# Turned tiles of a two-layer decoder trunk: one write to DRAM each in place of four, and VectorE's 32 x 32 squares taken from every fourth column

## The chip, the cores and the metric

The kernel runs on one core of a Trainium2 chip. The metric is the device time of one execution in microseconds (us). Engines are named as the profile names them: PE is TensorE, DVE is VectorE, ACT is ScalarE, POOL is GpSimd, and SP is SyncE, which here issues transfers and computes nothing. A transfer (DMA) is issued by SP, ACT or POOL and carried out by the core's 16 DMA engines.

## The reference

One sequence of 256 tokens with a width of 2048 goes through two layers in fp32. Each layer is a token mixer and an MLP, both behind an RMSNorm, both adding into the residual x:

```
h = rms_norm(x, mix_norm_g[i])
mix = fox_attention(h, ...) if i % 2 == 0 else dilated_attention(h, ...)
x = x + mix
h = rms_norm(x, mlp_norm_g[i])
a = relu(h @ w_up)               # 2048 -> 8192
x = x + (a * a) @ w_down         # 8192 -> 2048
```

The first mixer is causal softmax attention with 16 heads of 128 and a forget-gate bias. The second mixes three groups of 8 heads, each over a dilated window, with shared values. In both, q and k are normalised per head of 128 and scaled by a gain per column. Nearly all arithmetic lies in matrix products of 256 tokens with weights that are read from DRAM once.

## The kernel before

**Products.** Tokens lie in two tiles of 128 (`t`), columns in chunks of 512 (`NC`). To keep fp32 accuracy every operand is split in a rounded part (`wh`, `hT`, `aTh`) and the rest (`wl`, `aTl`), and each product is three matmuls: high x high, high x low, low x high (lines 471 to 473; in the wide products 1198 to 1200). A weight unit is 256 rows x 512 columns. SP loads it into a `raw` tile, ACT rounds it into `wh` (line 417) and DVE subtracts to get `wl` (line 418). There are five `wh` and five `wl` tiles, so ACT and DVE can be at most five units ahead of PE. In the up projections of the MLPs some pairs of column chunks are computed together, in what the code calls "wide" products: seven block products in place of eight, for which DVE also forms sums and differences of weights (`sd`, `v`, lines 414, 420 and 421). Such a unit costs DVE more than a plain one.

**Turning.** A product needs its left operand with the contracted dimension on the partitions, so activations are transposed between products. After the first norm, tiles are turned without PE. DVE's transpose takes a 128 x 512 tile as 32 x 32 squares: a square stays on its 32 partitions. To move it to other partitions, the tile is written to DRAM in four transfers, one for each 32 partitions, and read back by one transfer in which a partition reads 2 KB in one run. This is done in four places: the norms before the MLPs and the second mixer (`transposed_by_dma`, transpose on line 571), q and k (`qk_chain`, line 748), the softmax weights (`p_turned`, line 819, tiles of 128 x 384), and the squared activations of both MLPs (`turn_up`, line 1119). In the first three, SP issues the writes and the read, by `move`. In `turn_up` POOL issues the writes (line 1113) and SP the read. What comes back is split by ACT (line 1144) and DVE (lines 1148 and 1151) into `aTh` and `aTl`.

**Gains.** `more_constants` loads the gains of q and k (8 rows of 128) and of the MLP norms (32 rows) as rows, PE turns them into columns (line 212), DVE copies them to `gain` (line 213).

**Order.** The order on each engine is the order in which the program is written. `Jobs` weaves it: the products call `jobs.tick()` after every 128 rows of weights, and a chain such as `turn_up` is a generator that gives the number of ticks, or the event, after which it goes on. The same ticks hold before and after the change. Every engine works its queue in order; an instruction that waits holds up those behind it. In the order of DVE a transpose of `turn_up` stands between the weight splits, as in:

```
for t in range(NT):
    tiles.append(work.tile([P, NC], F32, tag="w", name=f"turned_{key}_{n}_{t}", bufs=6))
    nc.vector.transpose(...)      # DVE, line 1119
    if t:
        write(t - 1)              # POOL, line 1113
    yield 1                       # one tick: about six matmuls, and a weight split behind each second
```

Of the kernel before, what the change touches and what calls it, by code (L numbers as in the profile page):

```python
# [137 lines left out]
def trunk(ctx: ExitStack, tc, x, fox_w_in, fox_b_f, fox_q_gain, fox_k_gain, fox_w_out, dil_w_in,  # L138
# [94 lines left out]
    def more_constants():  # L233
        yield 5
        wf = work.tile([P, KC, FH], F32, tag="t2", name="wf")
        nc.sync.dma_start(wf, fox_w_in[0][:, 3 * D:3 * D + FH].rearrange("(c p) n -> p c n", p=P))
        nc.sync.dma_start(bf, fox_b_f.to_broadcast([P, FH]))
        rows = gain_rows("g_rest", [fox_q_gain, fox_k_gain, dil_q_gain[0], dil_k_gain[0],
                                    mlp_norm_g.rearrange(per_chunk, p=P)])
        di = distances()  # L240
        yield 9
        nc.scalar.copy(wfs[:, :, 0:FH], wf)
        nc.vector.tensor_sub(wfs[:, :, FH:2 * FH], wf, wfs[:, :, 0:FH].bitcast(F32))
        jobs.done.add("wf")
        yield 1
        gain_columns("g_rest", rows, FOX_G)
        for c in (FOX_G, DIL_G, DIL_G + 1, DIL_G + 2):
            nc.vector.tensor_scalar_mul(gain[:, c:c + 1], gain[:, c:c + 1], SCALE)
        yield 1
        mask = work.tile([P, 3 * P], F32, tag="t0", name="mask")  # L250
        nc.vector.tensor_copy(mask, di)
        nc.vector.tensor_scalar(mask, mask, 0.0, None, ALU.is_ge)
        nc.vector.tensor_scalar(mask, mask, BIG, -BIG, ALU.mult, ALU.add)
        tables["mask"] = mask
        jobs.done.add("mask")
# [117 lines left out]
    def move(dst, src):  # L373

        nc.sync.dma_start(dst, src)

    state = {"raw": 0, "split": 0}
    pooled, corners = [0], {"free": False, "users": []}
# [179 lines left out]
    def transposed_by_dma(tag, col, n):  # L558
# [3 lines left out]
        for t in range(NT):  # L562
# [4 lines left out]
                tile_ = both.rearrange("p a b -> p (a b)")[:, t * NC:(t + 1) * NC]  # L567
            else:
                tile_ = work.tile([P, NC], F32, tag="w", name=f"turned_{tag}_{n}_{t}", bufs=6)
            blocks = dram.tile([4, 32, 4, P], F32, tag="blocks", name=f"blocks_{tag}_{n}_{t}", bufs=4)  # L570
            nc.vector.transpose(tile_.rearrange("p (j b r) -> p b j r", j=4, b=4),
                                xt[n][:, t, :].rearrange("p (b j c) -> p b j c", j=4, c=32))
            for i in range(4):
                move(blocks[:, :, i, :].rearrange("j c x -> c j x"),
                     tile_[32 * i:32 * i + 32].rearrange("p (j x) -> p j x", j=4))
            tiles.append((tile_, blocks))
        yield 3
        for tile_, blocks in tiles:
            move(tile_, blocks.rearrange("j c i x -> (j c) (i x)"))
        yield 11 if n else 9  # L580
        for half in range(2):
            pr = n * 2 + half
# [140 lines left out]
    def qk_chain(acc, tag, key, parts):  # L723
# [17 lines left out]
        for t in range(NT):  # L741
# [7 lines left out]
            blocks = dram.tile([4, 32, 4, P], F32, tag="blocks", name=f"blocks_{key}_{t}", bufs=4)  # L749
            for i in range(4):  # L750
                move(blocks[:, :, i, :].rearrange("j c x -> c j x"), sq[t][32 * i:32 * i + 32].rearrange("p (j x) -> p j x", j=4))
            qn.append(q)
            turns.append(blocks)
            yield 2
        yield 1
        for t in range(NT):
            yield 2 * t
            move(qn[t], turns[t].rearrange("j c i x -> (j c) (i x)").rearrange("p (h d) -> p h d", h=4))
        yield clear(6)
        for t in range(NT):  # L760
            subs = []
# [53 lines left out]
    def p_turned(p, name, landing):  # L815


        turned = work.tile([P, 4, 3, 32], F32, tag="s", name=f"turned_{name}", bufs=S_BUFS)
        nc.vector.transpose(turned.rearrange("p j b r -> p b j r"), p.rearrange("p (b j c) -> p b j c", b=3, c=32))
        blocks = dram.tile([4, 32, 4, 3 * 32], F32, tag="pblocks", name=f"pblocks_{name}", bufs=4)  # L820
        for i in range(4):
            move(blocks[:, :, i, :].rearrange("j c x -> c j x"),
                 turned[32 * i:32 * i + 32].rearrange("p j b r -> p j (b r)"))
        yield 5
        move(turned.rearrange("p i b r -> p (i b r)"), blocks.rearrange("j c i x -> (j c) (i x)"))
        yield clear(landing)
        return turned

# [274 lines left out]
    def turn_up(rows, key, n, aT, free=None, behind=None):  # L1103
# [5 lines left out]
        held, tiles = [], []  # L1109

        def write(t):
            for i in range(4):
                nc.gpsimd.dma_start(held[t][:, :, i, :].rearrange("j c x -> c j x"),
                                    tiles[t][32 * i:32 * i + 32].rearrange("p (j x) -> p j x", j=4))

        for t in range(NT):
            tiles.append(work.tile([P, NC], F32, tag="w", name=f"turned_{key}_{n}_{t}", bufs=6))
            held.append(dram.tile([4, 32, 4, P], F32, tag="held", name=f"held_{key}_{n}_{t}", bufs=16))
            nc.vector.transpose(tiles[t].rearrange("p (j b r) -> p b j r", j=4, b=4),
                                rows[t].rearrange("p (b j c) -> p b j c", j=4, c=32))  # L1120
            if t:
                write(t - 1)
            yield 1
# [5 lines left out]
        for t in range(NT):  # L1129
            yield 1  # L1130
            back.append(work.tile([P, NC], F32, tag="w", name=f"back_{key}_{n}_{t}", bufs=6))
            move(back[t], held[t].rearrange("j c i x -> (j c) (i x)"))
        yield clear(more(6, "turned", *at, 2))
        if free:
            yield free
# [242 lines left out]
```

## Time and profile before

Three runs gave a median of 2074.55 us (2074.14 to 2074.99). The profiled execution took 2072.56 us itself; its trace spans 2070.5 us.

| | before |
|---|---|
| median of the runs | 2074.55 us |
| profiled execution | 2072.56 us, span 2070.5 us |
| PE busy | 2064.7 us |
| DVE busy | 1782.1 us, of which 96 to 99% in parts of the MLPs |
| ACT busy | 1328.4 us |
| POOL busy | 247.6 us |
| transfers | 549.51 MB, mean 265 GB/s |

Rows of a timeline give the start, the duration, the engine, the line of the kernel, the operation, and `out<-in` by the program's names. Rows of a group give the count (x), then the busy time in us, the mean duration of one in ns, and the idle time of the engine just before them. Rows of a window table give the busy time in that stretch, the number of instructions (x), the granted clock of PE, the share of DMA time and the rate of the transfers. Matmuls are pipelined: one of 512 columns is shown with 0.38 us, and the next one starts 0.215 or 0.216 us after it. So PE counts as busy also across a short wait, and a short wait shows only in the distance between two starts. The time from one stage of the trace to another is told by lines: lines 571 belong to norms, 748 and 819 to the mixers, 1119 to the MLPs (`n1` is the first MLP, `n3` the second).

### The profile page before, as it was taken

How to read it: one execution, taken by the hardware profiler on the slowest of the kernel's cores; microseconds unless marked ns; L12 is line 12 of the kernel's file. 1: busy time of each engine (PE TensorE's matmuls, PEld its weight loads, DVE VectorE, ACT ScalarE, POOL GpSimd, SP SyncE). 2: the span in 40 equal slices, each digit the busy share in tenths (PEclk: the TensorE clock that was granted, in tenths of full speed). 3: DMA queues.
4: the chain of work that ended last, by engine and by line, in shares of the span. 5: the costliest groups of instructions: out<-in, count | busy, mean ns of one | idle time of the engine just before them, and what ended most of it. 6: DMA issues, size and time to landing. Idle time of an engine off the chain costs nothing.

```text
span 2070.5 us, 29000 instructions
## 1 busy us (share of the span) xinstructions
PE 2064.7 (100%) x9790; PEld 1813.2 (88%) x9790; DVE 1782.1 (86%) x2283; ACT 1328.4 (64%) x1833; POOL 247.6 (12%) x367
## 2 busy tenths in 40 slices
PE   9999999999999999999999999999999999999999
PEld 7888888888888888888888888888888888888888
DVE  6888876899999999997768787767999899999984
ACT  6665654867676676765656565555866676676673
POOL 1000000022020211211010010000112020120230
PEclk9999999999999999999999999999999999999999
DMA  8888887889898989989877876877888898899995
GB/s 259 258 260 263 258 249 217 268 284 293 267 298 266 290 271 300 306 256 283 287 240 233 251 234 216 255 217 241 263 288 284 270 298 265 280 292 295 292 280 187
DMA packets 355924, 549.51 MB, mean 265 GB/s; under 512 B 43496, under 2 KB 131904, under 8 KB 355776
## 3 DMA queue, kind: packets, MB, share of 16 engines
q1 hardware_dynamic: 336512, 511.28, 76.5%
q0 software_dynamic: 18560, 35.67, 7.4%
q8 instruction: 76, 1.25, 0.2%
q10 hardware_dynamic: 704, 0.72, 0.1%
q14 instruction: 72, 0.59, 0.1%
HBM read 488.29 MB, written 40.39 MB: 255 GB/s over the span
## 4 chain that ended last, share of the span: by engine, by line
PE 99%; DMA 0%; SPq 0%; DVE 0%; issue 0%
PE acc L471 25%; PE acc L472 25%; PE acc L473 25%; PE wide_n_tp L1199 3%; PE wide_n_tp L1200 3%; PE wide_n_tp L1198 3%; PE wide_n_sc L1199 2%; PE wide_n_acc L1198 2%; PE wide_n_acc L1200 2%; PE wide_n_sc L1200 2%; PE wide_n_acc L1199 2%; PE wide_n_sc L1198 2%; PE sc_d L859 0%; PE sc_f L859 0%; PE po_f L808 0%; PE po_d L808 0%
## 5 line engine op out<-in xcount | busy, mean ns | idle before, releaser
L418 DVE TENSOR_TENSOR wl<-raw,wh 128x1024 fp32r<-128x1024 f32 (+1 forms) x755 | 910.0, 1213 | 227.8 <-ACT wh L417 219.6
L417 ACT CAST wh<-raw 128x1024 fp32r<-128x1024 f32 (+1 forms) x755 | 782.0, 1044 | 424.5 <-PE acc L473 333.2
L471 PE MATMUL acc<-wh,hT_n 128*128 128x512 f32 x864 | 328.7, 380 | 0.0
L472 PE MATMUL acc<-wl,hT_n 128*128 128x512 f32 x864 | 327.9, 379 | 0.0
L473 PE MATMUL acc<-wh,hT_n 128*128 128x512 f32 x864 | 327.8, 379 | 0.0
L472 PE MATMUL acc<-wl,aTh_n1a 128*128 128x512 f32 x512 | 194.2, 379 | 0.0
L471 PE MATMUL acc<-wh,aTh_n1a 128*128 128x512 f32 x512 | 194.2, 379 | 0.0
L473 PE MATMUL acc<-wh,aTl_n1a 128*128 128x512 f32 x512 | 194.2, 379 | 0.0
L417 ACT CAST wh<-sd 128x1024 fp32r<-128x1024 f32 x96 | 100.7, 1049 | 139.9 <-DVE sd L414 129.0
L473 PEld LDWEIGHTS acc<-wh,hT_n 128*128 128x128 f32 x864 | 163.5, 189 | 22.9
L472 PEld LDWEIGHTS acc<-wl,hT_n 128*128 128x128 f32 x864 | 163.7, 189 | 22.1 <-DVE wl L418 0.3
L471 PEld LDWEIGHTS acc<-wh,hT_n 128*128 128x128 f32 x864 | 163.6, 189 | 21.8
L473 PE MATMUL acc<-wh,aTl_n3a 128*128 128x512 f32 x480 | 182.1, 379 | 0.0
L471 PE MATMUL acc<-wh,aTh_n3a 128*128 128x512 f32 x480 | 182.1, 379 | 0.0
L472 PE MATMUL acc<-wl,aTh_n3a 128*128 128x512 f32 x480 | 182.1, 379 | 0.0
L1051 POOL DMA_DIRECT2D x<-y_n x72 | 64.0, 927 | 638.8 <-ACT y_n L1050 637.0
L417 ACT CAST wh<-v 128x1024 fp32r<-128x1024 f32 x96 | 100.7, 1048 | 44.2 <-PE acc L473 22.2
L418 DVE TENSOR_TENSOR wl<-v,wh 128x1024 fp32r<-128x1024 f32 x96 | 116.7, 1216 | 5.5 <-ACT wh L417 5.4
L418 DVE TENSOR_TENSOR wl<-sd,wh 128x1024 fp32r<-128x1024 f32 x96 | 116.7, 1216 | 0.0
L414 DVE TENSOR_TENSOR sd<-raw,raw 128x1024 f32<-128x1024 f32 x96 | 116.6, 1214 | 0.0
L471 PE MATMUL acc<-wh,hc_n 128*128 128x512 f32 x288 | 109.4, 380 | 0.0
L472 PE MATMUL acc<-wl,hc_n 128*128 128x512 f32 x288 | 109.3, 379 | 0.0
(679 smaller groups left out, 3913.8 us busy)
## 6 DMA issues: line engine op xcount, KB each, us to landing
raw<-in_mlp_w_up_dram SPq DMA_DIRECT2D x304, 512.0 KB, 5.1
raw<-in_mlp_w_down_dram SPq DMA_DIRECT2D x256, 512.0 KB, 5.4
raw<-in_dil_w_in_dram SPq DMA_DIRECT2D x192, 256.0 KB, 3.5
raw<-in_fox_w_in_dram SPq DMA_DIRECT2D x95, 512.0 KB, 4.9
x<-y_n POOLq DMA_DIRECT2D x72, 256.0 KB, 6.5
raw<-in_fox_w_out_dram SPq DMA_DIRECT2D x32, 512.0 KB, 4.8
raw<-in_dil_w_in_dram SPq DMA_DIRECT2D x32, 512.0 KB, 4.7
raw<-in_dil_w_out_dram SPq DMA_DIRECT2D x32, 512.0 KB, 4.4
```

The source lines that it names most:

```text
L414: nc.vector.tensor_sub(quarters[0], raw, raws[n - 1][:, 1, :].unsqueeze(1).to_broadcast([P, RAW_SUB, NC]))
L417: nc.scalar.copy(hi[:, part, :], raw[:, part, :])
L418: nc.vector.tensor_sub(lo[:, part, :], raw[:, part, :], hi[:, part, :].bitcast(F32))
L471: nc.tensor.matmul(acc[t], ah, hi, start=first, stop=False)
L472: nc.tensor.matmul(acc[t], ah, lo, start=False, stop=False)
L473: nc.tensor.matmul(acc[t], al, hi, start=False, stop=last)
L1051: nc.gpsimd.dma_start(xt[n][:, t, :], y, accum_op=ALU.add)
L1198: nc.tensor.matmul(banks[bank], ah, wh, start=what < 3 and of == 0, stop=False, **alone)
L1199: nc.tensor.matmul(banks[bank], ah, wl, start=False, stop=False, **alone)
L1200: nc.tensor.matmul(banks[bank], al, wh, start=False, stop=of == KC // 2 - 1, **alone)
```

## The change

In all four places the tile is now written to DRAM in one transfer of 128 partitions x 2 KB (1.5 KB for the softmax weights), as it lies. The reading transfer does the sorting: a partition reads four pieces of 512 bytes (384 for the softmax weights) that lie 32 rows apart. Read this way, partition p gets what came from old partitions with the index 4c + j in place of 32j + c. To have the columns in their old order, DVE's transpose now takes as one square's columns every fourth column of a 128-column block (`(b c j)` in place of `(b j c)`), on lines 571, 819 and 1119. For q and k the transpose on line 748 stays as it was, and the columns of a head come out in another order, the same one for q and k. Their gains are put in that order once: two small copies of DVE through a tile `spread`.

```diff
+        spread = work.tile([8, P], F32, tag="s", name="spread", bufs=S_BUFS)
+        nc.vector.tensor_copy(spread.rearrange("n (c j) -> n c j", j=4), rows[0:8].rearrange("n (j c) -> n c j", j=4))
+        nc.vector.tensor_copy(rows[0:8], spread)
         gain_columns("g_rest", rows, FOX_G)
...
+    def scratch(tag, name, width=P, bufs=4):
+        return dram.tile([P, 4 * width], F32, tag=tag, name=name, bufs=bufs)
+
+    def turned_back(blocks):
+        return blocks.rearrange("(i c) (j x) -> (c j) i x", i=4, j=4)
...
# transposed_by_dma
-            blocks = dram.tile([4, 32, 4, P], F32, tag="blocks", name=f"blocks_{tag}_{n}_{t}", bufs=4)
+            blocks = scratch("blocks", f"blocks_{tag}_{n}_{t}")
             nc.vector.transpose(tile_.rearrange("p (j b r) -> p b j r", j=4, b=4),
-                                xt[n][:, t, :].rearrange("p (b j c) -> p b j c", j=4, c=32))
-            for i in range(4):
-                move(blocks[:, :, i, :].rearrange("j c x -> c j x"),
-                     tile_[32 * i:32 * i + 32].rearrange("p (j x) -> p j x", j=4))
+                                xt[n][:, t, :].rearrange("p (b c j) -> p b j c", j=4, c=32))
+            move(blocks, tile_)
...
-            move(tile_, blocks.rearrange("j c i x -> (j c) (i x)"))
+            move(tile_.rearrange("p (i x) -> p i x", i=4), turned_back(blocks))
...
# qk_chain
-            for i in range(4):
-                move(blocks[:, :, i, :].rearrange("j c x -> c j x"), sq[t][32 * i:32 * i + 32].rearrange("p (j x) -> p j x", j=4))
+            move(blocks, sq[t])
...
# p_turned
-        nc.vector.transpose(turned.rearrange("p j b r -> p b j r"), p.rearrange("p (b j c) -> p b j c", b=3, c=32))
+        nc.vector.transpose(turned.rearrange("p j b r -> p b j r"), p.rearrange("p (b c j) -> p b j c", b=3, c=32))
...
# turn_up
-            for i in range(4):
-                nc.gpsimd.dma_start(held[t][:, :, i, :].rearrange("j c x -> c j x"),
-                                    tiles[t][32 * i:32 * i + 32].rearrange("p (j x) -> p j x", j=4))
+            nc.gpsimd.dma_start(held[t], tiles[t])
...
             nc.vector.transpose(tiles[t].rearrange("p (j b r) -> p b j r", j=4, b=4),
-                                rows[t].rearrange("p (b j c) -> p b j c", j=4, c=32))
+                                rows[t].rearrange("p (b c j) -> p b j c", j=4, c=32))
...
-            move(back[t], held[t].rearrange("j c i x -> (j c) (i x)"))
+            move(back[t].rearrange("p (i x) -> p i x", i=4), turned_back(held[t]))
```

No instruction of PE is added or removed, and the splits keep their order. POOL's order at the start of the first MLP, before the change; `held_n1a` is the DRAM copy of a turned tile, `x<-y` the added output of a down projection:

```order
L1113 DMA held_n1a_2_0_4582<-turned_n1a_2_0_4581 32x4x128 x4
L1113 DMA held_n1a_2_1_4600<-turned_n1a_2_1_4599 32x4x128 x4
L1113 DMA held_n1a_3_0_4877<-turned_n1a_3_0_4876 32x4x128 x4
L1113 DMA held_n1a_3_1_4890<-turned_n1a_3_1_4889 32x4x128 x4
L1051 DMA x_103<-y_n_0_0_194_5161 128x512
```

and with it:

```order
L1116 DMA held_n1a_2_0_4453<-turned_n1a_2_0_4452 128x512
L1116 DMA held_n1a_2_1_4471<-turned_n1a_2_1_4470 128x512
L1116 DMA held_n1a_3_0_4742<-turned_n1a_3_0_4741 128x512
L1116 DMA held_n1a_3_1_4755<-turned_n1a_3_1_4754 128x512
L1055 DMA x_103<-y_n_0_0_194_5020 128x512
```

Each write is one row in place of four (x4), at the same place. DVE's order about 29 us into the program, before the change, where it copies the turned gains out of PSUM (the brackets name what an instruction waits for):

```order
L418 TENSOR_TENSOR wl_384<-raw_245,wh_383 128x1024 [waits DMAHW1_49,Activation_49]
L243 TENSOR_TENSOR wfs<-wf,wfs 128x16x16 [waits DMAHW2_49,Activation_49]
L213 COPY gain<-ps_g_rest 128x40 [waits PE_49]
L248 TENSOR_SCALAR gain<-gain 128x1 [waits DVE_49]
L248 TENSOR_SCALAR gain<-gain 128x1 x3
```

and with it:

```order
L427 TENSOR_TENSOR wl_384<-raw_245,wh_383 128x1024 [waits DMAHW1_49,Activation_49]
L243 TENSOR_TENSOR wfs<-wf,wfs 128x16x16 [waits DMAHW2_49,Activation_49]
L247 COPY spread<-g_rest 8x128 [waits DMAHW6_49,DMAHW7_49,DMAHW5_49,DMAHW4_49]
L248 COPY g_rest<-spread 8x128 [waits DVE_49]
L213 COPY gain<-ps_g_rest 128x40 [waits PE_49]
```

The two copies stand ahead of the copy out of PSUM, and PE's transpose of the gains (line 212) now waits for them.

More of the change, by code (lines that the diff above doesn't have):

```diff
@@ L748, in qk_chain @@
             nc.vector.transpose(turned.rearrange("p j h r -> p h j r"), q.rearrange("p h (j c) -> p h j c", c=32))
-            blocks = dram.tile([4, 32, 4, P], F32, tag="blocks", name=f"blocks_{key}_{t}", bufs=4)
-            for i in range(4):
-                move(blocks[:, :, i, :].rearrange("j c x -> c j x"), sq[t][32 * i:32 * i + 32].rearrange("p (j x) -> p j x", j=4))
+            blocks = scratch("blocks", f"blocks_{key}_{t}")
+            move(blocks, sq[t])
             qn.append(q)
@@ L757, in qk_chain @@
             yield 2 * t
-            move(qn[t], turns[t].rearrange("j c i x -> (j c) (i x)").rearrange("p (h d) -> p h d", h=4))
+            move(qn[t], turned_back(turns[t]))
         yield clear(6)
@@ L818, in p_turned @@
         turned = work.tile([P, 4, 3, 32], F32, tag="s", name=f"turned_{name}", bufs=S_BUFS)
-        nc.vector.transpose(turned.rearrange("p j b r -> p b j r"), p.rearrange("p (b j c) -> p b j c", b=3, c=32))
-        blocks = dram.tile([4, 32, 4, 3 * 32], F32, tag="pblocks", name=f"pblocks_{name}", bufs=4)
-        for i in range(4):
-            move(blocks[:, :, i, :].rearrange("j c x -> c j x"),
-                 turned[32 * i:32 * i + 32].rearrange("p j b r -> p j (b r)"))
+        nc.vector.transpose(turned.rearrange("p j b r -> p b j r"), p.rearrange("p (b c j) -> p b j c", b=3, c=32))
+        blocks = scratch("pblocks", f"pblocks_{name}", 3 * 32)
+        move(blocks, turned.rearrange("p j b r -> p (j b r)"))
         yield 5
-        move(turned.rearrange("p i b r -> p (i b r)"), blocks.rearrange("j c i x -> (j c) (i x)"))
+        move(turned.rearrange("p i b r -> p i (b r)"), turned_back(blocks))
         yield clear(landing)
@@ L1111, in write @@
         def write(t):
-            for i in range(4):
-                nc.gpsimd.dma_start(held[t][:, :, i, :].rearrange("j c x -> c j x"),
-                                    tiles[t][32 * i:32 * i + 32].rearrange("p (j x) -> p j x", j=4))
+            nc.gpsimd.dma_start(held[t], tiles[t])
         for t in range(NT):
             tiles.append(work.tile([P, NC], F32, tag="w", name=f"turned_{key}_{n}_{t}", bufs=6))
-            held.append(dram.tile([4, 32, 4, P], F32, tag="held", name=f"held_{key}_{n}_{t}", bufs=16))
+            held.append(scratch("held", f"held_{key}_{n}_{t}", bufs=16))
             nc.vector.transpose(tiles[t].rearrange("p (j b r) -> p b j r", j=4, b=4),
-                                rows[t].rearrange("p (b j c) -> p b j c", j=4, c=32))
+                                rows[t].rearrange("p (b c j) -> p b j c", j=4, c=32))
             if t:
```

## The prediction

> **What bounds the kernel now.** I read the page's shares first, then PE's waits, then DVE by stretches of the first MLP, and last the timelines of DVE and PE side by side.
>
> ```profile
> PE 2064.7 (100%) x9790; PEld 1813.2 (88%) x9790; DVE 1782.1 (86%) x2283; ACT 1328.4 (64%) x1833; POOL 247.6 (12%) x367
> PE spare L193 <- DVE zeros L189: 1.1, 1, 1.1
> PE ptx_n L684 <- DMA x<-in_x_dram: 1.0, 1, 1.0
> 2000.00:2070.50 70.50, 66.81 (x356) 1.00 0.70 227
> 783.00:910.00 127.00, 126.00 (x132) 1.00 0.92 289
> 530.00:627.00 97.00, 90.65 (x95) 1.00 0.89 289
> ```
>
> PE is busy for 2064.7 of 2070.5 us. Of the 5.8 us that are left, its two listed waits take 2.1 us at the start, and 3.7 us (70.50 less 66.81, the fourth row) lie in the last stretch, at the end. The granted clock is 1.00. So between start and end PE hardly waits: there is nothing for fewer transfers to win there. The last two rows are DVE's busy time in two stretches of the first MLP: 126.00 of 127 us, and 90.65 of 97. DVE is the engine that is about to become the bound.
>
> How near it is shows the lead of a `wl`: the time from the end of DVE's row to the start of the first matmul that reads it. These are the smallest leads of the first MLP, each with DVE's row ahead of PE's:
>
> ```profile
> 421.37 1.18 DVE L418 TENSOR_TENSOR wl<-raw,wh 128x1024 fp32r<-128x1024 f32 x1
> 423.57 0.38 PE L472 MATMUL acc<-wl,hT_n 128*128 128x512 f32 x1
> 476.62 1.18 DVE L418 TENSOR_TENSOR wl<-raw,wh 128x1024 fp32r<-128x1024 f32 x1
> 479.25 0.38 PE L472 MATMUL acc<-wl,aTh_n1a 128*128 128x512 f32 x1
> 527.57 1.22 DVE L418 TENSOR_TENSOR wl<-sd,wh 128x1024 fp32r<-128x1024 f32 x1
> 529.76 0.38 PE L1199 MATMUL wide_n_sc<-wl,sums_n 128*128 128x512 f32 x1
> 624.40 1.22 DVE L418 TENSOR_TENSOR wl<-raw,wh 128x1024 fp32r<-128x1024 f32 x1
> 626.88 0.38 PE L472 MATMUL acc<-wl,aTh_n1a 128*128 128x512 f32 x1
> 697.20 1.22 DVE L418 TENSOR_TENSOR wl<-sd,wh 128x1024 fp32r<-128x1024 f32 x1
> 699.40 0.38 PE L1199 MATMUL wide_n_sc<-wl,sums_n 128*128 128x512 f32 x1
> 780.24 1.18 DVE L418 TENSOR_TENSOR wl<-sd,wh 128x1024 fp32r<-128x1024 f32 x1
> 782.28 0.38 PE L1199 MATMUL wide_n_sc<-wl,sums_n 128*128 128x512 f32 x1
> 908.09 1.22 DVE L418 TENSOR_TENSOR wl<-sd,wh 128x1024 fp32r<-128x1024 f32 x1
> 909.36 0.48 PE L1199 MATMUL wide_n_sc<-wl,sums_n 128*128 128x512 f32 x1
> ```
>
> Start less end gives 1.02, 1.45, 0.97, 1.26, 0.98, 0.86 and 0.05 us, 6.59 in all. At 909 us the lead is gone, and PE has already been held up a little there. Each low is the end of a run of wide products, in which a unit costs DVE more than PE; between two of them the lead recovers.
>
> **The change part by part.** *The writes.* POOL issues one for four in the MLPs, SP one for four elsewhere.
>
> ```profile
> L1113 POOL DMA_DIRECT2D held_n1a<-turned_n1a x128 | 71.5, 576 | 265.6 <-DVE turned_n1a L1119 253.2 <-DMA held_n1a<-turned_n1a 4.5 <-DMA x<-y_n 3.8
> held_n1a<-turned_n1a POOLq DMA_DIRECT2D x128, 64.0 KB, 4.9
> back_n1a<-held_n1a SPq DMA_DIRECT2D x32, 256.0 KB, 5.0
> x<-y_n POOLq DMA_DIRECT2D x72, 256.0 KB, 6.5
> ```
>
> Per layer 96 of 128 issues of 0.576 us go, 55 us of POOL, which mostly waits. A tile's last write was issued 3 x 0.576 = 1.73 us after its first and landed 4.9 us later, 6.6 in all. One write of 256 KB lands between 4.9 and 6.5 us after its issue (the small write and POOL's other 256 KB transfer): the read can go out 0.1 to 1.7 us earlier. That read now takes pieces of 512 bytes in place of 2 KB; the trace has no such read. I bound it by 1 us either way of its 5.0. POOL's later transfers stand behind these writes, and SP's weight loads behind these reads. Both come out near even, I take 0, and what hides it is PE's own work, since no wait of PE is for a load after the start.
>
> *The transposes.* This is where I see the price.
>
> ```profile
> L1119 DVE STREAM_TRANSPOSE turned_n1a<-c_n1a 128x512 f32<-128x512 f32 x24 | 16.5, 698 | 0.0
> 400.00:424.00 24.00, 2.81 (x4) 1.00 0.81 253
> ...
> 910.00:1000.00 90.00, 2.70 (x4) 1.00 0.88 276
> ```
>
> A transpose of 512 columns takes 0.70 us and now reads words that lie 16 bytes apart. The windows, cut at the lows above, hold four of them each: eight groups per MLP, all with DVE's queue of weight splits behind them, and PE behind the splits. No DVE row of before reads SBUF with such a hop. The nearest are the splits of q and k on line 777, 256 columns each and alike but for this: q is read in one run, k with every second word, 8 bytes apart. On ACT line 773 does the same.
>
> ```profile
> L777 DVE TENSOR_TENSOR f_0q<-sq_('fq', 2)_0_1786,f_0q x1: 384/384/384, 198.5 to 198.5; 128x256 fp32r<-128x256 f32 x1
> L777 DVE TENSOR_TENSOR f_0kl<-sq_('fk', 2)_0_2042,f_0kh x1: 492/492/492, 220.5 to 220.5; 128x256 fp32r<-128x256 f32 x1
> L773 ACT CAST f_0q<-sq_('fq', 2)_0_1786 x1: 411/411/411, 193.6 to 193.6; 128x256 fp32r<-128x256 f32 x1
> L773 ACT CAST f_0kh<-sq_('fk', 2)_0_2042 x1: 502/502/502, 216.9 to 216.9; 128x256 fp32r<-128x256 f32 x1
> ```
>
> A hop of two words costs DVE 108 ns per 256 columns (0.42 ns each) and ACT 91. Let d be what a transpose of 512 columns takes longer at a hop of four. Its ends are 0 (a transpose reads ahead, and hops are free to it) and 1.0 us, if a word's time goes with the hop: DVE's 1220 ns for 1024 columns (line 418) and 384 for 256 make 1.09 ns a word in one run, 1.51 at a hop of two, so 3.02 at four, and 512 x 1.93 ns is 0.99 us. Between: a hop of two would cost 0.22 for 512; if each doubling adds as much, 0.43; if each further word does, 0.65. These stay nearest to the row, and I take their middle, d = 0.54.
>
> [...]
>
> *What it costs.* A group adds 4d of DVE's time between two lows. What exceeds the lead at the low is time that PE waits; the lead then recovers. With 4d = 2.16 and the seven leads: 1.14, 0.71, 1.19, 0.90, 1.18, 1.30 and 2.11 us, 8.5 per layer. The eighth group, after 910 us, stands where DVE was busy 74.9 of 90 us, and costs nothing. The second MLP is the same program and has its own empty lead (below), so 17 us for both.
>
> ```profile
> 1978.34 0.48 PE L1199 MATMUL wide_n_sc<-wl,sums_n 128*128 128x512 f32 x1
> 910.00:1000.00 90.00, 74.91 (x104) 1.00 0.88 276
> 1100.00:1300.00 200.00, 200.00 (x991) 177.18 (x991) 157.78 (x236) 118.49 (x175) 14.17 (x7) 1.00 0.75 233
> L571 DVE STREAM_TRANSPOSE turned_n<-x 128x512 f32<-128x512 f32 x24 | 15.6, 687 | 0.0
> ```
>
> The transposes of norms (line 571, 24 of them) and of softmax weights pay the same d, in stages where DVE has slack: 157.78 of 200 us in the second mixer. Were that cover gone, the 24 would cost 13 us; I take 0, with up to 2 for the norms just ahead of an MLP.
>
> *The gains.* PE's transpose of the gains waits for two new copies.
>
> ```profile
> 28.84 0.42 DVE L243 TENSOR_TENSOR wfs<-wf,wfs 128x256 fp32r<-128x256 f32 x1
> 30.34 0.20 DVE L213 COPY gain<-ps_g_rest 128x40 f32<-128x40 f32 x1 [1.08 <-PE ps_g_rest L212]
> 30.05 0.25 PE L212 MATMUL ps_g_rest<-ident,g_rest 40*128 40x40 f32 x1
> ```
>
> DVE is free at 29.26 and PE comes at 30.05. Two copies of 8 x 128 take 0.2 us each by the COPY row, up to 0.4 for the hopping one: done by 29.7 to 29.9. I take 0; at worst 0.5 us, once.
>
> Sum: 2072.56 + 17 = 2089.6 us for an execution like the profiled one. The median of the runs stood 1.99 above it, so 2091.6 us, which I give as 2092.
>
> **The rivals.** *Hops are free to a transpose (not slower).* The place is line 1119, the price d, and it decides below d = 0.22: then 4d = 0.88 stays under the leads but for those at 782 and 909 us, and the sum is below 2 us for both layers. For it: line 777 reads two operands at once and a transpose reads one. Against: line 773 reads one too, and pays. Time: 2074.5 to 2076.5.
>
> *The time goes with the hop.* d = 1.0, 4d = 4.0, seven groups cost 28 less 6.6, the eighth perhaps 1: 22 per layer, 44 for both, 2118.6. For it: two engines of their own speeds pay nearly the same for the hop, 108 and 91 ns, as if SBUF set the time. [...]
>
> *The reads in small pieces come late.* Place: line 1144 on ACT, which holds up ACT's roundings behind it. 1 us on every group of a layer that is not covered would be 8 us per layer, 2090 with free transposes. Against: the earlier writes give back as much, and ACT is busy 64%.
>
> *Fewer issues help.* Between start and end PE can win only short waits such as those at 909 and 1978 us (0.48 us each where other rows have 0.38): a few tenths in all, so no less than 2073.5.
>
> **How the numbers follow.** What a measurement of this kernel can tell from no change is about 0.2%, 4.1 us. The forecast (d from 0.3 to 0.75, 2079 to 2103) gets 0.5, hops that go with the distance 0.2, free or nearly free hops 0.21, late reads alone 0.05, a gain 0.04. The single likeliest is 2092. The range, 2074 to 2117, leaves out most of the gain and the upper end of the second rival, some 0.15. The forecast's own range is 2079 to 2103. Slower by over 0.2% collects the forecast, the second rival and late reads, less a little at the forecast's lower edge: 0.74; within 0.2% the free hops and that edge: 0.22; faster 0.04.
>
> **What would show it.** Rows of the transposes of 512 columns near 1.24 us in place of 0.70, with those of q and k (line 748) unchanged, show the price; rows at 0.70 refute it. In PE's waits there should be `wl` and `wh` in the MLPs, at the ends of the wide runs, some 8 us per layer, and none in the mixers. POOL's busy time should fall by about 110 us and change nothing. I am wrong if the transposes stay at 0.70 us, or if they lengthen and PE still does not wait.

## The result and the profile after

The changed kernel takes 2119.12 us (median of 5 runs, 2117.17 to 2121.93), and the kernel before took 2074.99 us beside it (5 runs, 2074.14 to 2075.46): 1.0213 times as long, with a 95% interval from 1.0202 to 1.0223. The prediction said 2092, with a range from 2074 to 2117. The direction and the mechanism came as predicted, and the size was 2.6 times as large: 44 us in place of 17.

The page's busy time by engine, after the change:

```profile
PE 2081.7 (98%) x9790; PEld 1807.9 (85%) x9790; DVE 1864.9 (88%) x2285; ACT 1323.5 (63%) x1833; POOL 145.3 (7%) x175
```

VectorE's transposes, grouped by tile:

```profile
L1121 DVE STREAM_TRANSPOSE turned_n1a<-c_n1a 128x512 f32<-128x512 f32 x24 | 36.7, 1545 | 0.0
L580 DVE STREAM_TRANSPOSE turned_n<-x 128x512 f32<-128x512 f32 x24 | 36.3, 1566 | 0.0
L825 DVE STREAM_TRANSPOSE turned_f<-s_f 128x384 f32<-128x384 f32 x16 | 19.2, 1201 | 0.5
```

PE has the same 9790 matmuls, but its share falls from 100 to 98%: the span grew to 2117.4 us and the new time is idle time. POOL's busy time falls from 247.6 to 145.3 us. VectorE's rises by 82.8 us, and the transposes account for it (their rows add up to 89 us more): 698 ns has become 1545 in the MLPs, 687 has become 1566 in the norms, 578 has become 1201 for the 384 columns of the softmax weights.

Where PE waits (engine, tile and line, what it waits for; us in all, times, longest), after the change:

```profile
PE wide_n_sc L1201 <- DVE wl L427: 13.3, 21, 2.0
PE acc L481 <- DVE wl L427: 7.3, 10, 1.0
PE wide_n_tp L1201 <- DVE wl L427: 3.9, 4, 1.2
PE acc L480 <- ACT aTh_n3a L1146: 1.7, 1, 1.7
PE acc L480 <- ACT aTh_n1a L1146: 1.4, 1, 1.4
```

35 waits, 24.5 us, are for `wl`, the part of a weight that VectorE subtracts; before the change there was none of them in the list. The view counts only time in which PE shows no matmul at all. Since a matmul of 512 columns is shown with 0.38 us and the next one starts after 0.216, each of these waits is about 0.16 us longer than listed, 5.6 us for 35.

PE's clock has a part too. Behind the two waits for `aTh` the granted clock falls to 0.50 for 3.4 us, and matmuls start every 0.43 us. Three rows of PE at the first of them, and the window of that stretch (PE's busy time, granted clock, DMA share and GB/s):

```profile
968.26 0.79 PE L480 MATMUL acc<-wh,aTh_n1a 128*128 128x512 f32 x1 [1.41 <-ACT aTh_n1a L1146]
968.85 0.63 PE L481 MATMUL acc<-wl,aTh_n1a 128*128 128x512 f32 x1
969.27 0.63 PE L482 MATMUL acc<-wh,aTl_n1a 128*128 128x512 f32 x1
968.20:971.50 3.30, 3.24 (x8) 0.50 1.11 360
```

Such a stretch costs 1.7 us (eight matmuls, each 0.21 us late). The profiled execution before the change has none until its last 3 us. Not every wait has one behind it: there is none behind the wait of 2.0 us for `wl` at 798 us.

PE runs its 9790 matmuls in the same order before and after, so the starts of the same matmul can be compared. The last one starts 46.9 us later. Of these, 23.7 us come between 375 and 975 us of the time before (the first MLP with the norm ahead of it), 2.2 in the norm behind it, 20.8 from 1480 us on (the second MLP with its norm), 0.2 in the first 15 us, and nothing in the rest.

The waits lie where VectorE was full already. Two stretches of the timeline, after (busy time of PE, PE's weight loads, VectorE, ScalarE and POOL, then clock, DMA share and GB/s), and below them the first of the two before:

```profile
785.00:885.00 100.00, 96.41 (x443) 83.10 (x442) 99.62 (x100) 66.70 (x80) 12.71 (x17) 1.00 0.92 282
1050.00:1480.00 430.00, 430.00 (x2091) 379.29 (x2090) 332.40 (x467) 252.16 (x389) 24.07 (x13) 1.00 0.75 237
```

```profile
785.00:885.00 100.00, 100.00 (x465) 87.69 (x464) 99.11 (x104) 69.38 (x81) 17.48 (x26) 1.00 0.95 301
```

In the first MLP VectorE was busy for 99.11 of 100 us before; it cannot do more, so PE does less: 443 matmuls in place of 465. In the second mixer, where VectorE has slack, PE does not lose anything.

### The profile page after: what moved, and what is told of

Its sections match the earlier page's. It is cut to its first block, busy times and chain, and to the rows that moved or that the text cites. A ratio compares the mean times of both kernels' runs of the same rounds, so it can differ in the third digit from the quotient of the medians.

```text
span 2117.4 us, 28333 instructions
## 1 busy us (share of the span) xinstructions
PE 2081.7 (98%) x9790; PEld 1807.9 (85%) x9790; DVE 1864.9 (88%) x2285; ACT 1323.5 (63%) x1833; POOL 145.3 (7%) x175
## 4 chain that ended last, share of the span: by engine, by line
PE 50%; issue 26%; DVE 15%; ACT 3%; DMA 3%; POOL 2%; SPq 0%; DVEq 0%; POOLq 0%; ACTq 0%
PE acc L481 14%; PE acc L480 14%; PE acc L482 14%; DVE wl L427 8%; DVE turned_n1a L1121 2%; DVE sd L423 2%; ACT wh L426 1%; POOL x L1055 1%; DVE turned_n L580 1%; ACT room_n L599 1%; DVE v L429 1%; DMA turned_n<-blocks_n 1%; PE wide_n_tp L1202 1%; PE wide_n_tp L1200 1%; PE wide_n_tp L1201 1%
## 5 line engine op out<-in xcount | busy, mean ns | idle before, releaser
L481 PEld LDWEIGHTS acc<-wl,aTh_n1a 128*128 128x128 f32 x512 | 97.2, 190 | 18.1 <-DVE wl L427 4.5
L480 PEld LDWEIGHTS acc<-wh,aTh_n1a 128*128 128x128 f32 x512 | 97.2, 190 | 16.7 <-ACT aTh_n1a L1146 1.7
```

The costliest lines, as they stand in the source:

```text
L480: nc.tensor.matmul(acc[t], ah, hi, start=first, stop=False)
L481: nc.tensor.matmul(acc[t], ah, lo, start=False, stop=False)
```

## Hop or transfers: three runs

The change couples two things, a hop of four words in what the transposes read and another shape of writes and reads. The first run makes the hop alone, the second the transfers alone.

```diff
# hop alone: the kernel before, norms (571) and MLPs (1119); softmax weights (819) alike
-                                rows[t].rearrange("p (b j c) -> p b j c", j=4, c=32))
+                                rows[t].rearrange("p (b c j) -> p b j c", j=4, c=32))
```

> The kernel before with nothing changed but the columns that VectorE's squares take in the norms, the MLPs and the softmax weights: every fourth one, as in the changed kernel. The four writes, the block layout in DRAM and the reads stay as before (the features then stand in another order than the weights' rows expect: that part of the computation is changed). Theory (the hop alone makes the loss: the 512-column transposes take 1.54 us in place of 0.70, and PE waits for the weight halves that VectorE splits behind them): the 512-column rows at 1.5 to 1.6 us, 2115 to 2122 us, VectorE's busy time near 1865 us, POOL's near 248. Rival (the single write, or the read in 512-byte pieces, lands late and makes the loss): 2074 to 2080 us even with rows of 1.54 us.

2122.36 us (4 runs) against 2075.6 for the kernel before beside it: 1.0224, interval 1.0208 to 1.0239. The page's busy time by engine:

```profile
PE 2082.2 (98%) x9790; PEld 1807.9 (85%) x9790; DVE 1865.4 (88%) x2283; ACT 1325.4 (63%) x1833; POOL 250.3 (12%) x367
```

The largest group of PE's waits:

```profile
PE wide_n_sc L1199 <- DVE wl L418: 13.3, 20, 2.0
```

The time lies just above the expected span. The hop alone makes all of the loss, with the same 13.3 us at the wide products. POOL has its 367 instructions again and that does not matter.

```diff
# transfers alone: the changed kernel, the same three lines the other way
-                                rows[t].rearrange("p (b c j) -> p b j c", j=4, c=32))
+                                rows[t].rearrange("p (b j c) -> p b j c", j=4, c=32))
```

> The changed kernel with neighbouring columns again in the squares of norms, MLPs and softmax weights; the single writes and the reads in 512-byte pieces stay (the features then stand in another order than the weights' rows: that part of the computation is changed). Theory (the hop is all of the loss): rows of 0.70 us for 512 columns, 2073.5 to 2076 us, VectorE near 1782 us, POOL near 145 us. Rival (writes and reads have a part in it): 2080 us or more with rows of 0.70 us. Whether 96 fewer issues per layer win anything by themselves shows here too: PE's 99.7% leaves at most 1.5 us.

2078.36 us (10 runs) against 2075.6: 1.0008, interval 0.9999 to 1.0017. No gain from fewer issues, as forecast; the time lies between the theory's 2076 and the rival's 2080. A small loss cannot be told from none by the times, but PE has waits that the kernel before does not have. The two longest:

```profile
PE acc L480 <- ACT aTh_n3a L1146: 1.4, 1, 1.4
PE acc L480 <- ACT aTh_n1a L1146: 0.9, 1, 0.9
```

And a read is slower; the last figure of a transfer's row is the median from issue to landing, 5.1 us before:

```profile
back_n3a<-held_n3a SPq DMA_DIRECT2D x32, 256.0 KB, 5.9
```

Is it the single write or the read in small pieces that is late? The third run writes in four again, into the new order:

```diff
+    def put(engine, blocks, tile_):
+        for i in range(4):
+            engine.dma_start(blocks[32 * i:32 * i + 32], tile_[32 * i:32 * i + 32])
...
-            nc.gpsimd.dma_start(held[t], tiles[t])
+            put(nc.gpsimd, held[t], tiles[t])
```

> The run with single writes and neighbouring columns again, but each tile is written by four transfers of 32 partitions each, into the same order in DRAM; the read still gathers 512-byte pieces (features in another order than the weights' rows: that part is changed). With single writes PE waited for the transposed activations of the last chunk of an MLP once in each layer (0.9 and 1.4 us in the row of waits), which the kernel before never does, and the time was 1.0008 of before, between 0.9999 and 1.0017. Theory (the read in small pieces is what lands late): these waits stay, 2076 to 2079 us. Rival (the single write is late, since one issue carries all 256 KB where four are spread): the waits go, 2074 to 2076 us.

2077.08 us (11 runs) against 2074.84: 1.0010, interval 1.0001 to 1.0018. PE's wait for the last chunk, and the reads:

```profile
PE acc L484 <- ACT aTh_n1a L1150: 0.4, 1, 0.4
```

```profile
back_n3a<-held_n3a SPq DMA_DIRECT2D x32, 256.0 KB, 5.5
back_n1a<-held_n1a SPq DMA_DIRECT2D x32, 256.0 KB, 5.7
```

The time does not move between one write and four; the wait for the last chunk shrinks in the first MLP and is not in the list for the second, so neither expectation about the waits holds as it stands. The new layout costs some 2 us by the medians with either way of writing, and the reads, 5.5 to 5.9 us in place of 5.0 and 5.1, are what the two runs have in common. That the reads make the 2 us is argued from that; the size is at the edge of what these runs resolve.

## VectorE's time, or a disturbed memory

A hop could also hurt the others: words 16 bytes apart might take SBUF accesses from PE or ScalarE. Doing each MLP transpose twice, without a hop, adds VectorE's time alone.

```diff
             nc.vector.transpose(tiles[t].rearrange("p (j b r) -> p b j r", j=4, b=4),
                                 rows[t].rearrange("p (b j c) -> p b j c", j=4, c=32))
+            nc.vector.transpose(tiles[t].rearrange("p (j b r) -> p b j r", j=4, b=4),
+                                rows[t].rearrange("p (b j c) -> p b j c", j=4, c=32))
```

> The kernel before with each of the MLPs' 64 transposes done twice, neighbouring columns both times: 0.69 us more of VectorE per transpose with no hop and no other change. Theory (it is VectorE's time, not the way in which the hop reads the memory, that makes PE wait): by the four transposes of a group, 4 x 0.69 = 2.76 us against leads of 0.05 to 1.45 us, between the prediction's formula (2.76 x 7 - 6.6 = 12.7 us a layer, 2098 us) and the measured loss scaled (44.5 x 0.69 / 0.85 = 36 us, 2111 us). Rival (reading words 16 bytes apart disturbs the other engines' reads of the same memory, and this makes PE wait): 2074 to 2080 us.

2104.64 us (4 runs) against 2075.6: 1.0141, interval 1.0126 to 1.0156. The group of the added transposes, and PE's longest waits:

```profile
L1121 DVE STREAM_TRANSPOSE turned_n1a<-c_n1a 128x512 f32<-128x512 f32 x24 | 17.1, 712 | 0.8
```

```profile
PE wide_n_sc L1201 <- DVE wl L418: 12.8, 19, 2.0
```

64 more transposes of 0.71 us, 45.6 us of VectorE, cost 29.0 us; PE waits for the same tile at the same line. The rival that looks to a disturbed memory would have had 2080 at most. Below, the hop in the MLPs alone adds 64 x 0.84 = 53.8 us and costs 33.2 us more than the transfers alone: 0.62 us lost per us added, and 0.64 here. VectorE's time is what counts, not the way it is spent.

## Where the loss lies

```diff
# the changed kernel; norms (580) and softmax weights (825) take neighbouring columns again
-                                xt[n][:, t, :].rearrange("p (b c j) -> p b j c", j=4, c=32))
+                                xt[n][:, t, :].rearrange("p (b j c) -> p b j c", j=4, c=32))
```

> The changed kernel with every fourth column in the MLPs' squared activations alone; norms and softmax weights take neighbouring columns again (their features then stand in another order than the weights' rows: that part is changed). The trace of the changed kernel shows about 3 us of PE's waits beside norms and none in the mixers. Theory (nearly all of the loss comes from the 64 transposes of the MLPs): 2113 to 2118 us. Rival (the norms' 24 and the softmax weights' 24 transposes weigh by their number, 0.85 and 0.62 us each, 35 of 90 us added on VectorE): 2098 to 2105 us.

2111.53 us (4 runs) against 2075.6: 1.0170, interval 1.0153 to 1.0187; 1.5 us below the theory's span, and far above that of a loss by number. The stretches at the entry and at the exit of the first MLP, first in this run, then in the changed kernel:

```profile
375.00:425.00 50.00, 50.00 (x233) 43.80 (x232) 46.76 (x70) 39.93 (x75) 3.15 (x5) 1.00 0.80 251
960.00:1050.00 90.00, 87.98 (x398) 75.89 (x397) 72.23 (x116) 53.02 (x88) 3.05 (x5) 0.98 0.87 279
```

```profile
375.00:425.00 50.00, 48.58 (x222) 40.85 (x220) 46.31 (x73) 39.83 (x80) 2.07 (x3) 1.00 0.72 222
960.00:1050.00 90.00, 86.60 (x389) 73.81 (x388) 75.04 (x108) 48.31 (x78) 2.33 (x4) 0.98 0.85 266
```

PE gets back 1.4 us of busy time at either end, where norms are turned, of the 7.0 us by which the spans differ (2117.4 less 2110.4). By the starts of the same matmuls, the whole change loses 3.8 us at the entry and 2.2 us at the exit, and this run nothing at either. Now the reverse, the hop in norms and softmax weights alone:

```diff
# the changed kernel; the MLPs (1121) take neighbouring columns again
-                                rows[t].rearrange("p (b c j) -> p b j c", j=4, c=32))
+                                rows[t].rearrange("p (b j c) -> p b j c", j=4, c=32))
```

> The changed kernel with neighbouring columns again in the MLPs' squared activations alone; norms and softmax weights keep every fourth column (the MLPs' features then stand in another order than the weights' rows: that part is changed). The reverse of the run with the hop in the MLPs alone, which was 1.0170 of before against 1.0213 for the whole change: 9 us are left for norms and softmax weights if losses add up. Theory (they add up, and the 9 us are norms inside and beside the MLPs): 2081 to 2086 us. Rival (norms and softmax weights are hidden by themselves and cost only where the MLPs have already used up the lead): 2075 to 2079 us.

2080.01 us (10 runs) against 2075.17: 1.0021, interval 1.0012 to 1.0030. PE's two largest waits:

```profile
PE acc L481 <- DVE wl L427: 1.8, 3, 0.9
PE acc L480 <- ACT aTh_n1a L1146: 1.3, 1, 1.3
```

The number lies between the two expectations. Of its 4.8 us, 2 to 3 are the new layout's, so the norms and softmax weights cost some 2 us by themselves, and 7 to 8 in the whole change, on top of MLPs that have used up the lead. Losses do not add up: slack that hides one edit is spent by the other. The medians alone hardly resolve that, but the entry of the first MLP shows it: from 375 to 424 us of the time before, the hop in norms and softmax weights alone loses 0.7 us, the hop in the MLPs alone nothing, and both together 3.8.

## The price of a hop

Three runs read other patterns. Every second column everywhere, timed:

```diff
# in all three places, h=2; the tiles are written in one piece
-                                rows[t].rearrange("p (b c j) -> p b j c", j=4, c=32))
+                                rows[t].rearrange("p (g c h) -> p g h c", h=2, c=32))
```

> The changed kernel with every second column in place of every fourth in the squares of norms, MLPs and softmax weights, single writes kept (features in another order than the weights' rows: that part is changed). Price, from the row of a hop of two in the kernel before (256 columns 384 to 492 ns): 512 columns at 0.90 to 0.92 us, 0.21 us more. Theory (the leads at which the weight halves reach PE have to be used up first): four transposes add 0.86 us against leads of 0.05, 0.86, 0.97, 0.98, 1.02, 1.26 and 1.45 us: under 1 us a layer, 2074 to 2080 us, while 84 extra us of VectorE made 44 us in the changed kernel, so that 21 by proportion would make 11. Rival (loss in proportion to the added time): 2085 to 2088 us.

2079.51 us (10 runs) against 2075.17: 1.0019, interval 1.0010 to 1.0028. The transposes of the first MLP, and PE's waits in the wide products:

```profile
L1120 DVE STREAM_TRANSPOSE turned_n1a<-c_n1a 128x512 f32<-128x512 f32 x24 | 20.2, 852 | 0.0
```

```profile
PE wide_n_sc L1199 <- DVE wl L427: 0.5, 2, 0.3
```

Cheaper than the 0.90 to 0.92 us read off line 777, and only 0.5 us of waits in the wide products: four times 0.155 us stays below all leads but the one of 0.05. The 4.3 us are, again, for the most part the new layout's.

```diff
# first MLP h=8, second h=16; norms in pairs, eight words apart; softmax weights written four apart
+            apart = 8 if key[1] == "1" else 16
+            ... rows[t].rearrange("p (g c h) -> p g h c", h=apart, c=32)
...
+            ... xt[n][:, t, :].rearrange("p (x j e) -> p j x e", j=4, e=2)
```

> One look at prices of reading patterns of the squares; the changed kernel, in which the squares of the first MLP take every eighth column, those of the second every sixteenth, those of the norms pairs of neighbouring columns eight words apart, and those of the softmax weights read neighbouring columns and write every fourth (features in another order: that part is changed). [...] Rival (time goes on growing with the distance): 2 to 3 us at eight, 4 to 6 us at sixteen. Rival for the pairs (a pair of neighbours goes at the full rate): 0.69 us. [...]

One run, 2084.09 us. The transposes of the first MLP, the second, the norms and the softmax weights:

```profile
L1121 DVE STREAM_TRANSPOSE turned_n1a<-c_n1a 128x512 f32<-128x512 f32 x24 | 26.5, 1116 | 0.0
L1121 DVE STREAM_TRANSPOSE turned_n3a<-c_n3a 128x512 f32<-128x512 f32 x24 | 25.6, 1076 | 0.0
L580 DVE STREAM_TRANSPOSE turned_n<-x 128x512 f32<-128x512 f32 x24 | 15.5, 684 | 0.0
L824 DVE STREAM_TRANSPOSE turned_f<-s_f 128x384 f32<-128x384 f32 x16 | 19.3, 1205 | 0.5
```

PE's largest group of waits:

```profile
PE wide_n_sc L1200 <- DVE wl L427: 4.1, 11, 0.7
```

The price does not grow with the distance, as the rival had it, nor does it stay the same beyond four words: for 512 columns, words eight apart (1.116 us) and sixteen apart (1.076) are cheaper than words four apart (1.545). Pairs at eight are free (0.684 us, 0.687 with no hop), and writing four apart costs what reading four apart does (1.205 and 1.201 us for 384 columns). One thing was open, since this run wrote its tiles in one piece and the changed kernel writes scattered blocks. A second run crosses the two, and adds three patterns:

```diff
# first MLP: h=4, written in one piece; second: h=8, written in scattered blocks;
# norms: pairs four apart; forgetting attention: h=3; dilated: written eight apart
+                nc.vector.transpose(tiles[t].rearrange("p (g h r) -> p g h r", h=4, r=32), rows[t].rearrange("p (g c h) -> p g h c", h=4, c=32))
...
+                nc.vector.transpose(tiles[t].rearrange("p (h g r) -> p g h r", h=8, r=32), rows[t].rearrange("p (g c h) -> p g h c", h=8, c=32))
```

> A second look at prices (features in other orders: that part is changed). The squares of the first MLP: every fourth column, written as one contiguous tile; of the second MLP: every eighth column, written in a scattered order of blocks of 32; norms: pairs of neighbours four words apart; forgetting attention's softmax weights: every third column (384 columns); the dilated one's: neighbouring columns read, every eighth written. So far 512 columns took 0.85 (two apart), 1.54 (four), 1.12 (eight) and 1.08 us (sixteen). Theory (16 bytes between single words is a distance of its own, worse than 32 or 64): 1.5 us, 1.1 us, 0.69 us, 0.70 to 0.85 us, and 0.80 to 0.95 us. Rival (the order in which the blocks are written made the difference, since in the run of prices they were written in one piece): 1.0 to 1.1 us for every fourth, 1.5 us for every eighth.

Its groups of transposes, one run of 2103.93 us:

```profile
L1124 DVE STREAM_TRANSPOSE turned_n1a<-c_n1a 128x512 f32<-128x512 f32 x24 | 36.7, 1544 | 0.0
L1126 DVE STREAM_TRANSPOSE turned_n3a<-c_n3a 128x512 f32<-128x512 f32 x24 | 26.5, 1115 | 0.0
L580 DVE STREAM_TRANSPOSE turned_n<-x 128x512 f32<-128x512 f32 x24 | 19.4, 851 | 0.0
L825 DVE STREAM_TRANSPOSE turned_f<-s_f 128x384 f32<-128x384 f32 x16 | 14.2, 887 | 0.5
L827 DVE STREAM_TRANSPOSE turned_d<-p_d 128x384 f32<-128x384 f32 x8 | 7.1, 889 | 0.3
```

The order of the blocks does nothing (1544 and 1115 ns, 1545 and 1116 in the other order): single words 16 bytes apart stay the dearest that were measured. Pairs four apart are not free (0.851 us), against my expectation, and every third column (0.887 us) lies above the 0.70 to 0.85 that I expected. The added time per word (a row less its row without hop, over its columns):

| pattern, fp32 words | ns per word more |
|---|---|
| single, 2 apart | 0.30 |
| single, 3 apart | 0.80 |
| single, 4 apart, read or written | 1.65, 1.63 |
| single, 8 apart, read or written | 0.81, 0.81 |
| single, 16 apart | 0.74 |
| pairs, 4 apart | 0.32 |
| pairs, 8 apart | 0 |

## Two ways round the hop

If only VectorE's hop costs, the sorting can be done elsewhere. Here PE does it, whose matmuls read their weight columns in a woven order anyway (column n, then n + 256):

```diff
+    def in_turn_up(w):
+        return w.rearrange("p (h x j) -> p j x h", h=2, j=4)
...
-            wh, wl = (in_turn(w[:, i, :]) for w in (hi, lo))
+            wh, wl = (in_turn_up(w[:, i, :]) for w in (hi, lo))
```

> The kernel before with single writes for the MLPs alone (64 in place of 256 on POOL's queue) and the reads that gather four pieces, as in the changed kernel; but the features are brought into the order that this needs by TensorE: the matmuls of the up projections read their weight columns four apart, so that VectorE's squares take neighbouring columns again. Norms and softmax weights as before; nothing of the computation is left out. Theory (only VectorE's hop costs; the matmuls already read every second column from 256 words away at 0.216 us for 512 columns): 512-column transposes of the MLPs 0.70 us, matmuls of line 1199's successor unchanged at 0.215 to 0.217 us, 2073.5 to 2078 us, VectorE 1782 us. Rival (a hop of four costs TensorE too, as it costs VectorE): the up projections' matmuls grow; 1% on a third of 9790 matmuls is already 7 us, 2082 us and more.

2727.8 us (5 runs) against 2075.17: 1.3145, interval 1.3127 to 1.3163. Three rows of PE's timeline (start, duration), the last matmul of a down projection and two of the wide ones behind it:

```profile
801.82 0.38 PE L478 MATMUL acc<-wh,aTl_n1a 128*128 128x512 f32 x1
...
802.47 0.64 PE L1203 MATMUL wide_n_tp<-wl,hT_n 128*128 128x512 f32 x1
802.92 0.64 PE L1204 MATMUL wide_n_tp<-wh,hT_n 128*128 128x512 f32 x1
```

The group of an MLP's transposes:

```profile
L1122 DVE STREAM_TRANSPOSE turned_n1a<-c_n1a 128x512 f32<-128x512 f32 x24 | 16.6, 699 | 0.0
```

The rival was right, and by far more than its 1%: these matmuls start every 0.45 us in place of 0.216, at a granted clock of 1.0 over the run, and some 2800 of them make the 652 us. PE pays for a hop of four like VectorE (1.545 us in place of 0.698). What it read at 0.216 us is another pattern: n, n + 256, n + 1 and so on comes back to the same neighbours. I had seen a jump of 256 words and taken all jumps to cost no more.

The other way uses the free pattern: pairs of neighbours, eight apart, and two writes in place of one.

```diff
+        for e in range(2):
+            engine.dma_start(blocks[:, :, e, :], tile_[e::2].rearrange("p (j x) -> p j x", j=4))
...
+        return t.rearrange("p (x j e) -> p j x e", j=4, e=2)      # the transposes' source
...
+        return blocks.rearrange("(i c) j e x -> (c j e) i x", i=4)      # the read
```

> The changed kernel with pairs of neighbouring columns, eight columns apart, in all its squares, and two writes for each turned tile (the even partitions, then the odd ones) in place of one; read back in one transfer of 512-byte pieces, features in their own order, nothing of the computation left out. Theory (a pair of neighbours costs VectorE nothing, as the one look with 0.684 us for 512 columns showed; the transfers cost nothing either): 512-column transposes 0.68 to 0.71 us, 384 columns 0.57 to 0.59, POOL's busy time near 180 us, 2074 to 2079 us, as with single writes and neighbouring columns (1.0008 of before). Rival (writes from every second partition are slower and the reads land late): 2082 us or more, with PE waiting for the transposed activations. A gain over before is not expected: PE's 99.7% leave 1.5 us.

2086.84 us (5 runs) against 2074.91: 1.0053, interval 1.0039 to 1.0067. The pairs are free, and the whole was not. The norms' transposes with the idle time ahead of them, and PE's largest wait:

```profile
L587 DVE STREAM_TRANSPOSE turned_n<-x 128x512 f32<-128x512 f32 x24 | 15.8, 690 | 15.6 <-DMA blocks_n<-turned_n 15.6
```

```profile
PE acc L488 <- DVE wl L434: 3.4, 3, 1.8
```

In the norms VectorE stood still twice, for 15.6 us, until a write of theirs had landed, and PE waited for `wl` behind it. By the starts of the same matmuls these two stops cost PE 2.1 and 1.1 us. They are not the whole: the waits for the last chunk cost 1.9 us in the first MLP and 2.4 in the second, and behind the second stands another stretch at half clock, 1.7 us. What in the two writes makes it so was not tried. With the pairs in the MLPs alone, and the rest as in the kernel before:

```diff
# the kernel before, MLPs alone
-            for i in range(4):
-                nc.gpsimd.dma_start(held[t][:, :, i, :].rearrange("j c x -> c j x"),
-                                    tiles[t][32 * i:32 * i + 32].rearrange("p (j x) -> p j x", j=4))
+            for e in range(2):
+                nc.gpsimd.dma_start(held[t][:, :, e, :], tiles[t][e::2].rearrange("p (j x) -> p j x", j=4))
```

> The kernel before with pairs of neighbouring columns, eight apart, and two writes of every second partition in the MLPs alone: 128 POOL issues in place of 256, nothing else changed and nothing left out. With pairs everywhere the time was 1.0053 of before, and VectorE had stood still twice for 8 us in the norms until a write of theirs had landed. Theory (that loss is the norms'; the MLPs' pairs are free): transposes at 0.70 us, no wait for the weight halves over 0.4 us, 2074 to 2079 us. Rival (the MLPs' writes of every second partition cost it): 2080 us or more, with PE waiting for the transposed activations for 2 us and more in each layer.

2076.86 us (12 runs) against 2074.84: 1.0006, interval 0.9998 to 1.0015. An MLP's transposes, and PE's waits for the last chunks:

```profile
L1118 DVE STREAM_TRANSPOSE turned_n1a<-c_n1a 128x512 f32<-128x512 f32 x24 | 16.6, 699 | 0.5 <-DMA held_n1a<-turned_n1a 0.5
```

```profile
PE acc L471 <- ACT aTh_n3a L1144: 1.2, 1, 1.2
PE acc L471 <- ACT aTh_n1a L1144: 1.0, 1, 1.0
```

The theory holds for the MLPs: half of their writes go for no time that can be measured, and for no gain. That the norms make the rest of the loss of pairs everywhere is not shown, since q, k and the softmax weights were written in two as well. No version here is faster than the kernel before.

## Why the prediction missed

**PE as the bound: right.** POOL's busy time fell by 102 us (about 110 were forecast), and fewer issues alone won nothing: 1.0008.

**Writes and reads at net 0: 2 to 3 us short.** The reads grew by 0.2 to 1.0 us, inside the bound of 1 us, but the last chunk of each MLP has no cover for it: PE waits there in the run with the transfers alone, and not before the change.

**The price of a transpose: the step that failed.** d was taken as 0.54 us, "the middle" of two ways to draw on from a hop of two, and it measured 0.84 to 0.85 in the MLPs. All three rules I weighed (by doubling, by further word, with the distance) let the price rise with the hop; the table shows it highest at four words and half of that at eight, and one point could not tell such a course. Even that point was high for a transpose, 0.22 us where 0.155 came. The span of 0.3 to 0.75 us that the forecast gave to d was an estimate that no run shows: the hop of four lies above it, the hop of two below.

**From the price to the loss: right at most lows, with two terms missing.** The sum of "four d less the lead at the low", over seven groups and two layers, against what the runs showed; of the runs with the new layout I take off the 2.8 us of the transfers alone. The measured values carry the noise of two medians, some 2 us and more, and the second row is a single run:

| run | d, us | by the prediction's sum | measured |
|---|---|---|---|
| every second column | 0.155 | 1.1 | 1.6 |
| every eighth, every sixteenth | 0.42, 0.38 | 9.1 | 6.2 |
| transposes twice | 0.71 | 26.7 | 29.0 |
| every fourth, MLPs alone | 0.84 | 33.9 | 33.2 |

With the right d it would have given 34 us. At d = 0.54 it gave 17: near the leads the loss grows faster than the price.

The totals agree better than their parts. Here is the first MLP low by low, by the starts of the same matmuls: what the sum gives and what the run lost since the low before, in us.

| up to the low at | lead | sum, d = 0.84 | hop in MLPs alone | sum, d = 0.42 | every eighth column |
|---|---|---|---|---|---|
| 424 | 1.02 | 2.3 | 0.0 | 0.7 | 0.0 |
| 479 | 1.45 | 1.9 | 2.5 | 0.2 | 0.0 |
| 530 | 0.97 | 2.4 | 1.8 | 0.7 | 0.4 |
| 627 | 1.26 | 2.1 | 2.2 | 0.4 | 0.5 |
| 699 | 0.98 | 2.4 | 2.6 | 0.7 | 0.8 |
| 782 | 0.86 | 2.5 | 2.3 | 0.8 | 1.0 |
| 909 | 0.05 | 3.3 | 5.0, of which 1.7 by half clock | 1.6 | 1.6 |
| eighth group, to 975 | | 0 | 4.4, of which 1.7 by half clock | 0 | 1.8 |

From the second low to the seventh the rule holds within 0.7 us. The first low lost nothing in these two runs (2.1 us with the transposes done twice); in the run of the MLPs alone VectorE came to that group 2.9 us earlier than before. The eighth group, priced at 0, did lose time, and the stretches at half clock, three in the run of the MLPs alone (5.1 us), are in no term. These errors go both ways, so that 33.2 stands so near to 33.9 is in part luck.

**Norms and softmax weights at 0, with up to 2: half right.** Alone they cost some 2 us; after MLPs that leave no lead, 7 to 8.

**The eighth group at 0: wrong.** In the changed kernel it lost 4.3 us in the first layer and 3.9 in the second, 1.7 of each by half clock. The transfers alone lost 1.4 and 2.0 there, the hop with the old transfers 1.5 and 0.4, so both have a part.

**The gains at 0: right.** Between 15 and 375 us of the time before, where their copies lie, no matmul falls back.

**The sum of the parts.** By the medians, 33 for the MLPs, 7 to 8 for norms and softmax weights on top, and 2 to 3 for the transfers make the 44. But the hop with the old transfers lost 46.8 us, no less than the whole change, so these runs do not settle the share of the transfers within the whole.

**The rivals.** "The time goes with the hop" named 2118.6 and came within 1 us of the result, though not by its reason: its d of 0.99 was too large, it left out the norms, and the price does not grow with the distance, as words eight and sixteen apart show (0.42 and 0.38 us, 0.84 at four). That its number came so near is luck. I gave it 0.2, and ended the range at 2117. That a transpose reads ahead, the ground for an end at d = 0, was not shown: every hop of single words that was measured cost it time, 0.15 us for 512 columns at the least.

## What to carry to other kernels

Where an engine is full in a stretch and another waits on it, price an edit by the lead at the low points, not by the engine's mean share; from the second low to the seventh that rule held here within 0.7 us each, at two prices. Look also at PE's clock behind the waits: here it fell to half for 3.4 us behind some of them. A stride's price is not to be drawn on from another stride (here 0.155 us at two words, 0.84 at four, 0.42 at eight): measure the very pattern, in a run that does nothing else. Before a layout is changed for fewer transfers, look whether anything waits for a transfer.

## What the hardware showed that I had not expected

A transpose on VectorE that takes single fp32 words 16 bytes apart needed 1.54 us for 512 columns, more than for words 8 bytes (0.85), 32 bytes (1.12) or 64 bytes apart (1.08), and writing them 16 bytes apart took as long as reading (1.205 and 1.201 us for 384 columns). Pairs of neighbours cost nothing at 32 bytes (0.684 us against 0.687 with no hop) and took 0.85 us at 16, where they cost as much as every second word: 0.164 and 0.155 us more than with no hop. What makes 16 bytes the dearest of these distances no run shows. PE is sensitive to how it reads the weights, too: 0.45 us in place of 0.216 per matmul of 512 columns when its reads go on by four words.
